# Attention scores in two passes of the rounded format, in a pool/attention/expert layer on one core

## The chip, the cores and the metric

The kernel runs on one core of one Trainium2 chip. The metric is the device time of one execution in microseconds (us). The kernel before takes 1535.73 us, the median of three runs (1535.3 to 1536.64).

## The reference, cut to what matters

One layer of a small diffusion transformer on 512 tokens of width 1024, with 256 context tokens. `x` and the context are normalised and modulated (scale and shift from `silu(c) @ ada_w`), multiplied by `w_in`, and split into a pooling half and q, k, v of eight attention heads of width 64. A query of a row sees 16 columns by 8 rows of neighbours, with a bias table, and all 256 context keys:

```python
s_loc = jnp.einsum('bwhd,biwjhd->bhwij', q_r, k_win).astype(jnp.float32) * scale + bias
s_ctx = jnp.einsum('bwhd,bchd->bhwc', q_r, k_ctx).astype(jnp.float32) * scale
s_all = jnp.concatenate([s_loc.reshape(B, H, GRID_W, n_loc), s_ctx], axis=-1)
prob = jax.nn.softmax(s_all, axis=-1)
```

The pooled half and the attention result go through `w_out` and back into `x`. After that comes a layer of 16384 experts, of which each token picks 16 per head by two sorted lists of keys; most of the kernel's time is there.

## The kernel before, in words

Numbers are float32. TensorE also takes a rounded float32 format, F32R. Large products are written as three matmuls in that format (`mm3`, L66 to L69): each operand is split into a rounded part (`hi`, a ScalarE copy) and the rest (`lo`, a VectorE subtraction), and hi·hi, hi·lo and lo·hi are summed in PSUM (`split`, L71; `load_split`, L82). The attention scores do not use this: they are plain float32 matmuls.

**Stages.** From the start to some 44 us the inputs are normalised and turned. From 44 to 174 us a loop over `g` in the order 4, 5, 6, 7, 0, 1, 2, 3 multiplies by eight column blocks of `w_in`: 4 and 5 give k, 6 and 7 give v, 0 and 1 the pooling half, 2 and 3 give q. The loop also builds the modulation rows chunk by chunk (`ada_more`, which chunk at which `g` is in `ADA_AT`). From 174 to about 256 us come 32 attention steps, one for each of four blocks of 128 queries and eight heads, with nine units of the `w_out` product (`out_unit`) mixed in by the table `units`. The rest of `w_out` and the second normalisation end near 306 us, and the expert layer fills the rest.

**k and q before.** `KT[j]` holds the keys of two heads in 128 partitions, for 512 tokens and 256 context keys, copied by ScalarE from PSUM (L437, L441). `QZ[j]` holds the queries of two heads in 128 partitions, each head in a copy of its own in which the other head's 64 rows were set to zero (L291, L292), scaled by -1/8 (`to_qz`). So one matmul over all 128 rows gives the scores of one head.

**One attention step before.** `scores` makes two float32 matmuls of 256 columns, local keys (L377, or L380 and L381 in the last block) and context keys (L383), into one PSUM bank ("S", two banks); one VectorE instruction adds the bias and finds the minimum of the negated scores (L389); ScalarE takes the exponential and its sum (L391). `turn`, two steps behind, transposes the 512 columns on TensorE (L463) into a bank of tag "T" (two banks) and ScalarE copies them out (L465). `values`, three steps behind, makes four float32 matmuls with v (L473). `BIA` holds nine bias tiles: one for each head and one of zeros for the context. The eight of the first three blocks are loaded at the start and the eight of the last block during the third; each is negated by ScalarE after its load (L369).

**What sets the order.** Outside the regions marked as scheduled by hand, a planner orders the instructions at build time, by the order of the program and by estimated times, and hands out buffers. Each engine then runs its list in that order. Loads of weights, biases and modulation chunks all stand in one list of DMA issues, SP's: an issue that waits for its buffer holds up those behind it. The expert layer is ordered by hand. Rings of buffers that the change touches: "raw" (3, loads of weights), "m8" (2: the context operands, later the pooled half and both parts of the third block of `w_out`), "cx" (2), "pool" (3, temporaries and the copies of L465), "xp" (4).

Of the kernel before, what the change touches and what calls it, by code (L numbers as in the profile page):

```python
# [6 lines left out]
F32 = mybir.dt.float32  # L7
# [3 lines left out]
I32 = mybir.dt.int32  # L11
# [41 lines left out]
def _build(tc, nc, es, A, out, taps):  # L53
# [28 lines left out]
    def load_split(src, t=None, pool=None):  # L82
        t = t or load_raw(src)
        hi = (pool or stream).tile([P, KC, 256], F32R, tag="m8" if pool else "whi", name="whi", bufs=2)
        lo = (pool or stream).tile([P, KC, 256], F32R, tag="m8" if pool else "wlo", name="wlo", bufs=2)
        split(t, hi, lo)
        return hi, lo
# [74 lines left out]
    QZ = [fp.tile([P, 2, SEQ], F32, name=f"qz{j}") for j in range(4)]  # L162
# [15 lines left out]
    def rstd_of(x, pool):  # L178
        st = pool.tile([P, 2], F32, tag="st", name="st", bufs=4)
        scr = pool.tile([P, D], BF, tag="pool", name="sq", bufs=3)  # L180
# [138 lines left out]
    ADA_AT = {6: 2, 7: 3, 1: 4, 3: 5}  # L319
# [10 lines left out]
    def pooling(g, x):  # L330
        w = WINDOWS[g]
        pw = fp.tile([P, P], F32, tag="pw", name="pw", bufs=2)
        nc.scalar.dma_start(pw, A["pool_w"][g])
        s = fp.tile([P, 528], F32, tag="pool", name="pl", bufs=3)
        nc.vector.tensor_add(s[:, 1:528], x[:, 0:527], x[:, 1:528])
        lo_, hi_ = 1, 528
        step = 1
        while step * 2 < w:
            s2 = fp.tile([P, 528], F32, tag="pool", name="pl", bufs=3)
# [6 lines left out]
        po = fp.tile([P, 512], F32, tag="pool", name="po", bufs=3)  # L346
# [26 lines left out]
    def scores(b, h):  # L373
        kt, qs = KT[h // 2], QZ[h // 2][:, h % 2, b * P:(b + 1) * P]
        sp = psf.tile([P, 512], F32, tag="S", name="ps")
        if b < 3:
            nc.tensor.matmul(sp[:, 0:256], qs, kt[:, b * P:b * P + 256], start=True, stop=True)  # L377
            kb = [b, b + 1, 4, 5]
        else:
            nc.tensor.matmul(sp[:, 0:128], qs, kt[:, 0:P], start=True, stop=True)  # L380
            nc.tensor.matmul(sp[:, 128:256], qs, kt[:, 384:512], start=True, stop=True)  # L381
# [5 lines left out]
        st = fp.tile([P, 1], F32, tag="ast", name="ast", bufs=6)  # L387
# [8 lines left out]
    def to_qz(jj, pt):  # L396
        for e in range(2):
            r = slice(e * 64, e * 64 + 64)
            act(QZ[jj][r, e, 0:384], pt[r, 64:448], AF.Copy, scale=-0.125)
            act(QZ[jj][r, e, 384:512].rearrange("p (a c) -> p a c", c=64), edges(pt[r, :]), AF.Copy, scale=-0.125)  # L400

    def early_scores():
        for n in range(H):
            ld_bias(n)
        for n in range(2):
            q1.append(scores(*steps[n]))

    for g in (4, 5, 6, 7, 0, 1, 2, 3):
# [15 lines left out]
        for k, j in order_kj(g):  # L424
            cs = slice(j * P, (j + 1) * P)
            if g == 3 and j == 1 and k == 0:
                to_qz(2, pzs[0])
                early_scores()
# [3 lines left out]
        for j in range(2):  # L432
# [3 lines left out]
            if sec == 2:  # L436
                act(KT[jj][:, :SEQ], pt, AF.Copy)  # L437
# [3 lines left out]
                act(KT[jj][:, SEQ:], pc[:, :CTX], AF.Copy)  # L441
            elif sec == 1:
                if jj != 2:
                    to_qz(jj, pt)
            else:
                xp = fp.tile([P, 528], F32, tag="xp", name="xp", bufs=4)
# [13 lines left out]
    def turn(b, h, pr, kb):  # L460
# [3 lines left out]
        pT = fp.tile([P, 528], F32, tag="pool", name="pT", bufs=3)[:, :512]  # L464
# [10 lines left out]
    def normalise(b):  # L475
        nc.vector.reciprocal(sums[b][:, 1, :], sums[b][:, 0, :])
        ob = fp.tile([P, 528], F32, tag="xp", name="ob", bufs=4)[:, :512]
# [16 lines left out]
    def out_unit(g, t):  # L494
# [6 lines left out]
        for k in range(KC):  # L501
            mm3(pt[:, :256], mixh[:, k, ts_], mixl[:, k, ts_],
                whi[:, k, :], wlo[:, k, :], k == 0, k == KC - 1)
# [66 lines left out]
    def scale2(t):  # L570
        st = fp.tile([P, 4], F32, tag="st2", name="st2", bufs=4)
        scr = fp.tile([P, D], BF, tag="pool", name="sq2", bufs=3)
# [141 lines left out]
    ED = persist.tile([P, P], I32, name="eD")  # L714
    GD = persist.tile([P, P], F32, name="gD")
# [185 lines left out]
    dots = persist.tile([P, P], F32, name="dots")  # L901
# [378 lines left out]
```

## Time and profile before

| what | value |
|---|---|
| median of three runs | 1535.73 us (1535.3 to 1536.64) |
| the profiled execution's own time | 1536.22 us |
| its span, first to last instruction | 1534.5 us |
| mean granted TensorE clock | 0.991 |
| busy: TensorE, weight loads, VectorE, ScalarE, GpSimd | 1502.8, 1347.2, 1203.8, 612.2, 343.3 us |

PE is TensorE's matmuls, PEld its weight loads (they run beside matmuls), DVE is VectorE, ACT ScalarE, SP the queue that issues DMAs. The recorded length of a matmul is more than what it costs in a row of matmuls, since they overlap: the price of one is read from start to start. A float32 matmul of the program shows as two records.

### The profile page before, as it was taken

The page shows a single profiled execution, that of the slowest core. Times are in us where ns is not written, and L with a number is a line of the kernel's source. Part 1 is how long each engine was busy: PE and PEld are TensorE (multiplying, and loading weights), DVE is VectorE, ACT ScalarE, POOL GpSimd, SP SyncE. Part 2 cuts the span into 40 slices and gives each one's busy share as a digit, 9 for nine tenths or more (in the row PEclk, how much of TensorE's full clock was granted, in tenths as well). Part 3 has the DMA queues.
Part 4 walks back from the last instruction along what each step waited for, and adds up shares of the span by engine and source line. Part 5 has one row for each costly group of instructions (what it writes and reads, how often), then busy time and mean ns, then how long its engine had stood idle before and what let it go on. Part 6 is the DMA issues. An engine that isn't in the chain of part 4 may idle for free.

```text
span 1534.5 us, 22100 instructions
## 1 busy us (share of the span) xinstructions
PE 1502.8 (98%) x8553; PEld 1347.2 (88%) x8553; DVE 1203.8 (78%) x2208; ACT 612.2 (40%) x893; POOL 343.3 (22%) x278
## 2 busy tenths in 40 slices
PE   7999999999999999999999999999999999999997
PEld 3897799888999999999898888898889889889886
DVE  7857533538999998976888888878888898888896
ACT  4423554423334455554333433423333333432343
POOL 0000000000000000000234435444445444444441
PEclk9999999999999999999999999999999999999999
DMA  9575300032235467877699999999999999998981
GB/s 378 183 279 208 114 25 5 28 120 94 99 125 189 178 230 291 319 299 275 219 359 383 348 354 351 379 314 354 345 362 336 372 359 373 331 349 321 375 300 56
DMA packets 136166, 398.25 MB, mean 260 GB/s; under 512 B 9334, under 2 KB 62198, under 8 KB 120828
## 3 DMA queue, kind: packets, MB, share of 16 engines
q1 hardware_dynamic: 92280, 225.10, 40.7%
q0 software_dynamic: 36864, 134.23, 23.7%
q10 hardware_dynamic: 6916, 37.49, 6.2%
q8 instruction: 67, 1.10, 0.3%
q14 instruction: 39, 0.32, 0.1%
HBM read 358.52 MB, written 38.28 MB: 259 GB/s over the span
## 4 chain that ended last, share of the span: by engine, by line
PE 53%; issue 8%; POOL 4%; DVE 3%; DMA 3%; ACT 1%; POOLq 0%; ACTq 0%; DVEq 0%
PE pa L69 9%; PE pa L67 9%; PE pa L68 9%; PE acc L67 8%; PE acc L68 8%; PE acc L69 8%; POOL gr L912 4%; DMA gr<-in_v,eD 3%; PE wp L853 3%; DVE wlo L553 1%; DVE gr L919 0%; ACT whi L547 0%; DVE gm L839 0%; DVE y L1073 0%; DVE y L1072 0%
## 5 line engine op out<-in xcount | busy, mean ns | idle before, releaser
L69 PE MATMUL pa<-h2hi,wlo 128*128 128x384 f32 (+1 forms) x1152 | 397.4, 345 | 3.8 <-DVE wlo L553 3.7
L67 PE MATMUL pa<-h2hi,whi 128*128 128x384 f32 (+1 forms) x1152 | 400.4, 348 | 0.0
L68 PE MATMUL pa<-h2lo,whi 128*128 128x384 f32 (+1 forms) x1152 | 396.7, 344 | 0.0
L67 PE MATMUL acc<-vh,wah 128*128 128x512 f32 x768 | 299.2, 390 | 1.4 <-ACT wah L1037 1.4
L68 PE MATMUL acc<-vl,wah 128*128 128x512 f32 x768 | 299.6, 390 | 0.0
L69 PE MATMUL acc<-vh,wal 128*128 128x512 f32 x768 | 298.8, 389 | 0.0
L912 POOL DMA_INDIRECT gr<-in_u,eD x128 | 158.7, 1240 | 520.4 <-ACT wah L1037 310.7
L69 PEld LDWEIGHTS pa<-h2hi,wlo 128*128 128x128 f32 x1152 | 217.6, 189 | 11.5 <-DVE wlo L553 5.5
L67 PEld LDWEIGHTS pa<-h2hi,whi 128*128 128x128 f32 x1152 | 217.8, 189 | 8.2
L68 PEld LDWEIGHTS pa<-h2lo,whi 128*128 128x128 f32 x1152 | 217.7, 189 | 8.0
L912 POOL DMA_INDIRECT gr<-in_v,eD x128 | 172.4, 1347 | 199.7 <-DVE accD L925 177.6
L925 DVE SCALAR_TENSOR_TENSOR accD<-gr,dots,accD 128x1024 f32<-128x1024 f32 x128 | 164.0, 1281 | 49.2 <-DMA gr<-in_v,eD 47.7
L919 DVE SCALAR_TENSOR_TENSOR gr<-gr,h2D 128x1024 f32<-128x1024 f32 x128 | 153.9, 1221 | 40.8 <-DMA gr<-in_u,eD 40.6
L553 DVE TENSOR_TENSOR wlo<-raw,whi 128x2048 fp32r<-128x2048 f32 x58 | 132.5, 2285 | 59.1 <-ACT whi L547 59.0
L69 PEld LDWEIGHTS acc<-vh,wal 128*128 128x128 f32 x768 | 144.2, 188 | 30.6 <-DVE wal L1044 0.3
L67 PEld LDWEIGHTS acc<-vh,wah 128*128 128x128 f32 x768 | 144.2, 188 | 29.8 <-ACT wah L1037 1.8
L68 PEld LDWEIGHTS acc<-vl,wah 128*128 128x128 f32 x768 | 144.1, 188 | 27.3
L1037 ACT ACTIVATE wah<-a 128x384 fp32r<-128x384 f32 x72 | 37.9, 526 | 203.4 <-DVE a L1035 203.3
L547 ACT ACTIVATE whi<-raw 128x2048 fp32r<-128x2048 f32 x58 | 110.8, 1910 | 14.4 <-ACT apair L685 6.3
L1019 ACT ACTIVATE vh<-raw 128x1024 fp32r<-128x1024 f32 x76 | 80.2, 1056 | 52.1 <-PE acc L69 52.0
L1026 DVE TENSOR_TENSOR vl<-raw,vh 128x1024 fp32r<-128x1024 f32 x76 | 92.5, 1217 | 1.2 <-ACT vh L1019 1.1
L1014 ACT ACTIVATE a<-pa 128x384 f32<-128x384 f32 x72 | 35.2, 489 | 118.6 <-PE pa L69 118.4
(260 smaller groups left out, 2071.3 us busy)
## 6 DMA issues: line engine op xcount, KB each, us to landing
raw<-in_u SPq DMA_DIRECT2D x50, 1024.0 KB, 5.0
raw<-in_v SPq DMA_DIRECT2D x38, 1024.0 KB, 9.5
vraw<-in_v SPq DMA_DIRECT2D x26, 1024.0 KB, 10.1
w_dram<-stg ACTq DMA_DIRECT2D x12, 2048.0 KB, 8.1
wt<-w_dram SPq DMA_DIRECT2D x32, 768.0 KB, 14.7
awr<-in_ada SPq DMA_DIRECT2D x16, 1024.0 KB, 4.8
vraw<-in_u SPq DMA_DIRECT2D x14, 1024.0 KB, 9.6
a_dram<-apair ACTq DMA_DIRECT2D x28, 384.0 KB, 3.7
```

The source lines that it names most:

```text
L67: nc.tensor.matmul(o, lh, rh, start=start, stop=False)
L68: nc.tensor.matmul(o, lh, rl, start=False, stop=False)
L69: nc.tensor.matmul(o, ll, rh, start=False, stop=stop)
L547: act(hi, raws[n], AF.Copy)
L553: nc.vector.tensor_sub(lo, raws.pop(n), parts[n][0].bitcast(F32))
L853: nc.tensor.matmul(wp[:, x, :], flat(ohj, 4 * q + x), flat(G[m], 4 * q + x), start=m == 0, stop=m == 1)
L912: nc.gpsimd.indirect_dma_start(out=r, out_offset=None, in_=A[kind], in_offset=bass.IndirectOffsetOnAxis(ap=ED[:, s:s + 1], axis=0))
L919: nc.vector.scalar_tensor_tensor(r, r, 1.0, h2D, op0=OP.mult, op1=OP.mult, accum_out=dots[:, s:s + 1])
L925: nc.vector.scalar_tensor_tensor(accD, r, wD[:, s:s + 1], accD, op0=OP.mult, op1=OP.add)
L1019: act(vh, vrs[seq[x]], AF.Copy)
L1026: nc.vector.tensor_sub(vl, vrs.pop(i), vs[i][0].bitcast(F32))
L1037: act(wah, avals[i], AF.Copy)
```

## The change

The rounded parts of the keys and the queries are made once, and the scores become two passes in F32R.

- `K2[h]`, one tile per head instead of one per two heads, holds the rounded key in the head's own 64 partitions and the rest of the key in the other 64. The rest is subtracted by VectorE into a temporary and moved across partitions by a DMA from SBUF to SBUF (`to_k2`). There are four `jj` and two parts (tokens, context), with two heads each: 16 copies, 16 subtractions and 16 DMAs in place of 8 copies.
- `QA[j]` holds the rounded query of each head twice, in both halves of the partitions (the second by a DMA); `QB` holds the rest of the query, in the head's own 64 partitions (`to_q`): 16 copies as before, 16 VectorE instructions and 8 DMAs more. The eight memsets of `QZ` go.
- A score is `QA · K2` over 128 rows, which sums rounded query times rounded key and rounded query times rest of key, plus `QB · K2` over the head's 64 rows. Four F32R matmuls of 256 columns take the place of two float32 matmuls of 256 columns; the last block's two pieces of 128 columns become one strided operand.
- The score has its own sign now: the maximum is found, and one small VectorE instruction negates it for the exponential. The bias needs no negation: its 16 ScalarE instructions go.
- `BIA` has three rotating tiles and the zeros. A bias is loaded for each of the 32 steps, three steps ahead.
- `xp` and `ob` move into the ring "pool", now of four buffers (seven in two rings before); `pw` has one buffer instead of two. `QB` takes one "m8" buffer, the third block of `w_out` has its rest in two "cx" buffers. Modulation chunk 5 is built at `g` 2 instead of 3. `ED`, `GD` and `dots` move to another pool.

```diff
     def load_split(src, t=None, pool=None):
...
+        if pool:
+            los = [pool.tile([P, KC // 2, 256], F32R, tag="cx", name="wlo2", bufs=2) for _ in range(2)]
+            act(hi, t, AF.Copy)
+            for n, lo in enumerate(los):
+                ks = slice(n * KC // 2, (n + 1) * KC // 2)
+                nc.vector.tensor_sub(lo, t[:, ks, :], hi[:, ks, :].bitcast(F32))
+            return hi, los
...
-    KT = [fp.tile([P, SEQ + CTX], F32, name=f"kT{j}") for j in range(4)]
-    for j in range(4):
-        nc.vector.memset(QZ[j][64:128, 0, :], 0.0)
-        nc.vector.memset(QZ[j][0:64, 1, :], 0.0)
+    K2 = [fp.tile([P, SEQ + CTX], F32R, name=f"k2_{h}") for h in range(H)]
+    QA = []
+    QB = []
+
+    def to_k2(jj, pt, dst, n):
+        lo = fp.tile([P, 512], F32R, tag="pr", name="klo", bufs=3)
+        for e in range(2):
+            h, r, o = 2 * jj + e, slice(e * 64, e * 64 + 64), slice(64 - e * 64, 128 - e * 64)
+            act(K2[h][r, dst], pt[r, :n], AF.Copy)
+            nc.vector.tensor_sub(lo[r, :n], pt[r, :n], K2[h][r, dst].bitcast(F32))
+            nc.sync.dma_start(K2[h][o, dst].bitcast(F32), lo[r, :n].bitcast(F32))
...
-    ADA_AT = {6: 2, 7: 3, 1: 4, 3: 5}
+    ADA_AT = {6: 2, 7: 3, 1: 4, 2: 5}
...
-    BIA = fp.tile([P, H + 1, 256], F32, name="bias")
-    nc.vector.memset(BIA[:, H, :], 0.0)
+    NB = 3
+    BIA = fp.tile([P, NB + 1, 256], F32, name="bias")
+    nc.vector.memset(BIA[:, NB, :], 0.0)
...
     def ld_bias(n):
         if n < len(steps):
             b, h = steps[n]
-            if b in (0, 3):
-                nc.sync.dma_start(BIA[:, h, :], A["bias"][h, b // 3])
-                act(BIA[:, h, :], BIA[:, h, :], AF.Copy, scale=-1.0)
+            nc.sync.dma_start(BIA[:, n % NB, :], A["bias"][h, b // 3])
...
     def scores(b, h):
-        kt, qs = KT[h // 2], QZ[h // 2][:, h % 2, b * P:(b + 1) * P]
+        k2, r = K2[h], slice(h % 2 * 64, h % 2 * 64 + 64)
+        qs = slice(b * P, (b + 1) * P)
+        qa, qb = QA[h // 2][:, h % 2, qs], QB[0][r, h // 2, qs]
...
-        nc.tensor.matmul(sp[:, 256:512], qs, kt[:, SEQ:SEQ + CTX], start=True, stop=True)
+        ol = sp[:, 0:256] if b < 3 else two(sp[:, 0:256])
+        for o, kk in ((ol, loc), (sp[:, 256:512], lambda z: z[:, SEQ:SEQ + CTX])):
+            nc.tensor.matmul(o, qa, kk(k2), start=True, stop=False)
+            nc.tensor.matmul(o, qb, kk(k2[r, :]), start=False, stop=True)
...
-        nc.vector.tensor_tensor_reduce(halves(pr), halves(sp), BIA[:, h::H - h, :], op0=OP.add, op1=OP.min,
-                                       scale=1.0, scalar=3.0e38, accum_out=st)
-        act(pr, pr, AF.Exp, bias=st, scale=-1.0, accum_out=sums[b][:, 0, h:h + 1])
+        i = steps.index((b, h)) % NB
+        nc.vector.tensor_tensor_reduce(halves(pr), halves(sp), BIA[:, i::NB - i, :], op0=OP.add, op1=OP.max,
+                                       scale=1.0, scalar=-3.0e38, accum_out=st[:, 0:1])
+        nc.vector.tensor_scalar(st[:, 1:2], st[:, 0:1], -1.0, None, op0=OP.mult)
+        act(pr, pr, AF.Exp, bias=st[:, 1:2], accum_out=sums[b][:, 0, h:h + 1])
...
-    def to_qz(jj, pt):
+    def to_q(jj, pt):
+        if not QB:
+            QA.extend(fp.tile([P, 2, SEQ], F32R, tag=f"qz{j}", name=f"qa{j}", bufs=1) for j in range(4))
+            QB.append(fp.tile([P, 4, SEQ], F32R, tag="m8", name="qb", bufs=2))
...
+                act(d(qa), z, AF.Copy, scale=0.125)
+                nc.vector.scalar_tensor_tensor(d(qb[r, :]), z, 0.125, d(qa.bitcast(F32)), op0=OP.mult, op1=OP.subtract)
+            nc.sync.dma_start(QA[jj][o, e, :].bitcast(F32), qa.bitcast(F32))
...
-            if n >= 2 * H:
-                ld_bias(n + H)
+            ld_bias(n + NB)
```

## Rows read from the trace of the kernel before

**Rows 1.** The page, parts 1 and 2: busy us of each engine; PE's busy tenths.
```profile
PE 1502.8 (98%) x8553; PEld 1347.2 (88%) x8553; DVE 1203.8 (78%) x2208; ACT 612.2 (40%) x893; POOL 343.3 (22%) x278
...
PE   7999999999999999999999999999999999999997
```
**Rows 2.** Stretches: us, busy us of PE, PEld, DVE, ACT, POOL, granted clock, DMA.
```profile
62.00:72.00 10.00, 10.00 (x56) 8.29 (x55) 8.83 (x16) 2.95 (x4) 0.00 (x0) 1.00 0.39 143
...
175.00:185.00 10.00, 8.83 (x61) 7.48 (x60) 9.21 (x12) 9.13 (x18) 0.00 (x0) 1.00 0.30 105
...
200.00:215.00 15.00, 15.00 (x116) 14.16 (x115) 5.23 (x15) 7.30 (x19) 0.00 (x0) 1.00 0.07 19
```
**Rows 3.** Timeline of PE over one attention step: start us, us, line, count.
```profile
199.26 0.65 PE L377 MATMUL ps<-kT,qz 128*128 128x256 f32 x2
199.75 0.59 PE L383 MATMUL ps<-kT,qz 128*128 128x256 f32 x2
200.18 0.60 PE L463 MATMUL tp<-small,pr 128*128 128x128 f32 x4
200.62 1.00 PE L473 MATMUL op<-vn,pT 128*128 128x64 f32 x8
201.46 0.65 PE L377 MATMUL ps<-kT,qz 128*128 128x256 f32 x2
```
**Rows 4.** Timeline of PE and PEld in a unit of the w_out product.
```profile
206.25 0.28 PE L67 MATMUL po<-whi,mixh 128*128 128x256 f32 x1
206.26 0.19 PEld L68 LDWEIGHTS po<-wlo,mixh 128*128 128x128 f32 x1
206.37 0.28 PE L68 MATMUL po<-wlo,mixh 128*128 128x256 f32 x1
...
208.59 0.28 PE L69 MATMUL po<-whi,mixl 128*128 128x256 f32 x1
```
**Rows 5.** Timeline of ACT where its work piles up as attention starts.
```profile
179.00 0.71 ACT L391 ACTIVATE pr<-pr,ast 128x512 f32<-128x512 f32 x1
...
181.50 0.72 ACT L391 ACTIVATE pr<-pr,ast 128x512 f32<-128x512 f32 x1
```
**Rows 6.** Timelines of PE, ACT and DVE as attention starts.
```profile
173.90 0.59 PE L377 MATMUL ps<-kT,qz 128*128 128x256 f32 x2
...
178.81 0.70 PE L377 MATMUL ps<-kT,qz 128*128 128x256 f32 x2 [0.94 <-DVE ast L389]
...
180.47 1.10 PE L473 MATMUL op<-vn,pT 128*128 128x64 f32 x8
...
161.75 1.93 ACT L72 ACTIVATE whi<-raw 128x2048 fp32r<-128x2048 f32 x1
...
177.18 1.91 ACT L456 ACTIVATE mixh<-psd 128x2048 fp32r<-128x2048 f32 x1
...
175.85 2.29 DVE L73 TENSOR_TENSOR wlo<-raw,whi 128x2048 fp32r<-128x2048 f32 x1 [0.20 <-ACT whi L72]
```
**Rows 7.** Groups by form, 0 to 420 us: busy us, mean ns, idle before.
```profile
L389 DVE CUSTOM_DVE_ANT_1 pr<-ps,bias 128x512 f32<-128x512 f32 x28 | 19.2, 690 | 26.8 <-PE ps L383 26.2 <-PE tp L463 0.6
...
L437 ACT ACTIVATE kT<-pz 128x512 f32<-128x512 f32 x4 | 2.4, 599 | 4.6 <-PE pz L69 4.5
...
L489 DVE TENSOR_TENSOR mixl<-pmix,mixh 128x512 fp32r<-128x512 f32 x4 | 2.8, 692 | 5.2 <-ACT mixh L488 5.2
...
L291 DVE MEMSET qz<- 64x512 f32 x4 | 1.9, 485 | 0.6 <-issue 0.2
```
**Rows 8.** Timeline of DVE in the key stage.
```profile
66.60 0.42 DVE L213 TENSOR_TENSOR clo<-vn,chi 128x256 fp32r<-128x256 f32 x1
...
79.28 0.75 DVE L128 TENSOR_SCALAR aacc<-awr,cc 128x1024 f32<-128x1024 f32 x1 [2.29 <-DMA awr<-in_ada]
```
**Rows 9.** The bias tile's 16 loads, from issue to landing.
```profile
DMA to landing us min/median/max: 2.0/2.2/3.2
```
**Rows 10.** Waits of SP's queue, 100 to 300 us: total, times, longest.
```profile
SPq L79 <- DVE wlo L73: 26.9, 4, 14.4
```

More of the change, by code (lines that the diff above doesn't have):

```diff
@@ L84, in load_split @@
         hi = (pool or stream).tile([P, KC, 256], F32R, tag="m8" if pool else "whi", name="whi", bufs=2)
-        lo = (pool or stream).tile([P, KC, 256], F32R, tag="m8" if pool else "wlo", name="wlo", bufs=2)
+        if pool:
[5 more added lines that the diff above has]
+            return hi, los
+        lo = stream.tile([P, KC, 256], F32R, tag="wlo", name="wlo", bufs=2)
         split(t, hi, lo)
@@ L161, in _build @@
     VN = [VNA[:, t, :] for t in range(6)]
-    QZ = [fp.tile([P, 2, SEQ], F32, name=f"qz{j}") for j in range(4)]
+    QZ = [fp.tile([P, 2, SEQ], F32, tag=f"qz{j}", name=f"qz{j}", bufs=1) for j in range(4)]
     hhi = persist.tile([P, KC, SEQ], F32R, tag="hhi", name="hhi")
@@ L338, in pooling @@
         while step * 2 < w:
-            s2 = fp.tile([P, 528], F32, tag="pool", name="pl", bufs=3)
+            s2 = fp.tile([P, 528], F32, tag="pool", name="pl", bufs=4)
             a, b = lo_ + step, hi_ - step
@@ L366, in ld_bias @@
             b, h = steps[n]
-            if b in (0, 3):
-                nc.sync.dma_start(BIA[:, h, :], A["bias"][h, b // 3])
-                act(BIA[:, h, :], BIA[:, h, :], AF.Copy, scale=-1.0)
+            nc.sync.dma_start(BIA[:, n % NB, :], A["bias"][h, b // 3])
     sums, ops = {}, {}
     def scores(b, h):
-        kt, qs = KT[h // 2], QZ[h // 2][:, h % 2, b * P:(b + 1) * P]
+        k2, r = K2[h], slice(h % 2 * 64, h % 2 * 64 + 64)
+        qs = slice(b * P, (b + 1) * P)
+        qa, qb = QA[h // 2][:, h % 2, qs], QB[0][r, h // 2, qs]
         sp = psf.tile([P, 512], F32, tag="S", name="ps")
+        two = lambda z: z.rearrange("p (a n) -> p a n", n=P)
         if b < 3:
-            nc.tensor.matmul(sp[:, 0:256], qs, kt[:, b * P:b * P + 256], start=True, stop=True)
+            loc = lambda z: z[:, b * P:b * P + 256]
             kb = [b, b + 1, 4, 5]
         else:
-            nc.tensor.matmul(sp[:, 0:128], qs, kt[:, 0:P], start=True, stop=True)
-            nc.tensor.matmul(sp[:, 128:256], qs, kt[:, 384:512], start=True, stop=True)
+            loc = lambda z: two(z[:, 0:512])[:, 0::3, :]
             kb = [0, 3, 4, 5]
-        nc.tensor.matmul(sp[:, 256:512], qs, kt[:, SEQ:SEQ + CTX], start=True, stop=True)
+        ol = sp[:, 0:256] if b < 3 else two(sp[:, 0:256])
+        for o, kk in ((ol, loc), (sp[:, 256:512], lambda z: z[:, SEQ:SEQ + CTX])):
+            nc.tensor.matmul(o, qa, kk(k2), start=True, stop=False)
+            nc.tensor.matmul(o, qb, kk(k2[r, :]), start=False, stop=True)
         if h == 0:
@@ L386, in scores @@
         pr = fp.tile([P, 512], F32, tag="pr", name="pr", bufs=3)
[L387 removed]
+        st = fp.tile([P, 2], F32, tag="ast", name="ast", bufs=6)
         halves = lambda z: z.rearrange("p (a n) -> p a n", n=256)
[L389 to L391 removed]
+        i = steps.index((b, h)) % NB
[3 more added lines that the diff above has]
+        act(pr, pr, AF.Exp, bias=st[:, 1:2], accum_out=sums[b][:, 0, h:h + 1])
         return b, h, pr, kb
     q1 = []
[L396 to L400 removed]
+    def to_q(jj, pt):
+        if not QB:
+            QA.extend(fp.tile([P, 2, SEQ], F32R, tag=f"qz{j}", name=f"qa{j}", bufs=1) for j in range(4))
+            QB.append(fp.tile([P, 4, SEQ], F32R, tag="m8", name="qb", bufs=2))
+        qb = QB[0][:, jj, :]
+        for e in range(2):
+            r, o = slice(e * 64, e * 64 + 64), slice(64 - e * 64, 128 - e * 64)
+            qa = QA[jj][r, e, :]
+            blk = lambda z: z.rearrange("p (a c) -> p a c", c=64)
+            for d, z in ((lambda t: t[:, 0:384], pt[r, 64:448]), (lambda t: blk(t[:, 384:512]), edges(pt[r, :]))):
+                act(d(qa), z, AF.Copy, scale=0.125)
+                nc.vector.scalar_tensor_tensor(d(qb[r, :]), z, 0.125, d(qa.bitcast(F32)), op0=OP.mult, op1=OP.subtract)
+            nc.sync.dma_start(QA[jj][o, e, :].bitcast(F32), qa.bitcast(F32))
     def early_scores():
[L403 removed]
+        for n in range(NB):
             ld_bias(n)
@@ L426, in _build @@
             if g == 3 and j == 1 and k == 0:
-                to_qz(2, pzs[0])
+                to_q(2, pzs[0])
                 early_scores()
@@ L436, in _build @@
             if sec == 2:
-                act(KT[jj][:, :SEQ], pt, AF.Copy)
+                to_k2(jj, pt, slice(0, SEQ), SEQ)
                 pc = psf.tile([P, 512], F32, tag="O", name="pz2")
@@ L440, in _build @@
                     mm3(pc[:, :CTX], whi[:, k, cs], wlo[:, k, cs], chi[:, k, :], clo[:, k, :], k == 0, k == KC - 1)
-                act(KT[jj][:, SEQ:], pc[:, :CTX], AF.Copy)
+                to_k2(jj, pc, slice(SEQ, SEQ + CTX), CTX)
             elif sec == 1:
                 if jj != 2:
-                    to_qz(jj, pt)
+                    to_q(jj, pt)
             else:
-                xp = fp.tile([P, 528], F32, tag="xp", name="xp", bufs=4)
+                xp = fp.tile([P, 528], F32, tag="pool", name="xp", bufs=4)
                 nc.vector.memset(xp[:, 0:8], 0.0)
@@ L713, in _build @@
                    allow_small_or_imprecise_dtypes=True)
-    ED = persist.tile([P, P], I32, name="eD")
-    GD = persist.tile([P, P], F32, name="gD")
+    ED = late.tile([P, P], I32, name="eD")
+    GD = late.tile([P, P], F32, name="gD")
     slots = {}
@@ L900, in _build @@
     accD = mp.tile([P, D], F32, name="accD")
-    dots = persist.tile([P, P], F32, name="dots")
+    dots = late.tile([P, P], F32, name="dots")
     wD = dots
```

16 lines of the change are left out of this document (8 added, 8 removed).

## The prediction

> **What bounds the kernel now.** I read the page first: TensorE is busy for 98% of the span, and in nine tenths or more of every slice but the first and the last [rows 1]. So whatever shortens TensorE's list shortens the kernel, if no other engine steps in. Then I asked for the stretches in which the change works. In the steady part of attention (200 to 215 us) TensorE is busy for all 15.00 us at a granted clock of 1.00, its 2.4 GHz level, while VectorE has 5.23 us of work and ScalarE 7.30. As attention starts (175 to 185) it is otherwise: VectorE 9.21 of 10 us, ScalarE 9.13, TensorE 8.83. In the key stage (62 to 72) TensorE is full and VectorE has 8.83 of 10 [rows 2]. The three stretches have different limits, so the change is priced in each by itself.
>
> The recorded length of a matmul says little, since matmuls overlap; I read from start to start. One step runs from 199.26 to 201.46, 2.20 us: 0.92 for the scores (two float32 matmuls of 0.43, and 0.06 at the start), 0.44 for four transposes, 0.84 for the values [rows 3].
>
> **The change part by part.** The sum is made against the profiled execution, 1536.22 us (span 1534.5 and 1.7 around it), which is 0.5 above the median of 1535.73.
>
> *The scores.* Two float32 matmuls go, four F32R matmuls of 256 columns come. Such matmuls stand in the `w_out` units: from 206.25 to 208.59 there are 20 of them from start to start, so 0.117 each, each with a weight load of its own [rows 4]. A step's scores then cost 4 x 0.117 + 0.06 = 0.53 instead of 0.92: 0.39 saved, 12.5 us in 32 steps, and a period of 1.81. Two of the four matmuls have only 64 rows, and no row shows that. Below, I bound them by one of the eight records of the values, 0.84 / 8 = 0.105 [rows 3], which would give 0.8 us more in all; above, by a float32 record of the same columns, 0.43 / 2 = 0.215, which takes 64 x 0.098 = 6.3 us back. I take 0.117, since columns, format and load are the same and only the rows differ. The last block's operand in one strided piece is taken at the same price.
>
> A rule speaks against this change here. The rows show a weight load of 0.19 us begun at 206.26, while the matmul begun at 206.25 is still on record, and the next matmul 0.12 after the last: a load of the whole array runs beside a matmul of the whole array [rows 4]. The Trainium skill (TensorE: Matmul & The Clock Gate, section "The mechanism") says that a weight load overlaps with matmuls in flight only when their row groups differ. By that rule the trace does not agree for full loads; for a 64-row load between full ones no row here shows it. What it would make of the time is a rival below.
>
> *Do ScalarE and VectorE keep up with 1.81?* When ScalarE has a pile of work, two steps of it (an exponential and a copy each) take from 179.00 to 181.50, 1.25 a step [rows 5]. VectorE has 0.69 for L389 [rows 7]; reading out the result and the new negation of one column are two small instructions, which I estimate at 0.3 together. The transposes come two steps behind the scores, 3.6 us, and the chain between (1.0 on VectorE, 0.9 on ScalarE, some 0.6 of hand-over) is 2.5. So the steady part stays TensorE's, and the saving is real there.
>
> *The start of attention.* Here part of it is lost. TensorE waits for VectorE at 178.81, behind a split of 2.29 us begun at 175.85, and begins the first values at 180.47, since ScalarE had 1.91 us of `mixh` at 177.18 [rows 6]. The four and a half steps of scores done between 173.90 and 180.47 are not what this waits for, so their 4.5 x 0.39 = 1.7 us come back as idle time. The bank of the last q block is held longer by a VectorE instruction on 64x384: 0.5 by columns from the 0.69 of L489, which bounds it above [rows 7]; below, 0. I take 0.5. The ScalarE split of the third `w_out` block stood at 161.75; now its buffer is free only after the instructions on the pooled half, `mixh` at 177.18 and the one after it [rows 6]. That is 1.9 us in the middle of ScalarE's pile: 0 if it falls beside a `w_out` unit, 1.9 without slack. I take 1.3.
>
> *The key stage.* ScalarE's copies grow from 8 to 16, of 0.60 and less [rows 7], some 4 us more on an engine with 2.95 in 10 [rows 2]: nothing. VectorE gets 16 subtractions, 8 of 0.69 (as L489) and 8 of 0.42 (as L213), 8.9 us, less eight memsets of 0.485, 3.9 [rows 7, 8]: 5.0 net. VectorE delivers the last context operand at 66.60 and later waits 2.29 us for a DMA [rows 8]; that and the memsets' place cover most of it. The first four subtractions fall before 66 us and hold both "S" banks some 2 to 3 us longer, while TensorE has context products to do. Bounds: 0, and 2.8 us if the four are paid in full. I take 0.7.
>
> *The queries* add 16 VectorE instructions, 8 of some 0.5 and 8 smaller, from 150 to 175 us; the next product in TensorE's list covers them, and without that cover they would cost some 6 us. I take nothing but the 0.5 above. The bias negations that go, the smaller ring for pooling, the moved modulation chunk and the single `pw` buffer change only what stands beside that product: nothing, and 1 us lost at most, if a pooling copy is late.
>
> *DMAs.* 24 moves within SBUF and 32 bias loads (16 before) stand in SP's list. A bias is issued after L389 of three steps before and lands in 2.2 us, at most 3.2 [rows 9]; three steps of 1.81 are 5.4, less 0.8 for L389: some 2 us to spare. For a move no row stands; I take the same 2.2, which only the last q block waits for, beside VectorE's and ScalarE's piles. 0.3 for both together; the upper end is the first rival.
>
> *Sum:* 12.5 - 1.7 - 0.5 - 1.3 - 0.7 - 0.3 = 8.0 us. What follows is TensorE's and starts earlier by that [rows 1]. So 1528.2 in a profiled execution, 1527.7 against the median.
>
> **The rivals.**
> - *SP's list blocks the biases.* Loads of the next weights stand in the same list and wait for their buffers: four of them waited 26.9 us in all, the longest 14.4 [rows 10]. Should the planner put such a load ahead of a bias that is needed soon, the scores stop until it is released. It decides from the 2 us of slack on; a wait of 14.4 in the wrong place costs 12.4, and the time is 1527.7 + 12.4 = 1540. For it: the list runs strictly in order, and the moves of the last q block stand in it too. Against: the planner orders by when it expects buffers to be free, and TensorE has few gaps by that order now.
> - *Weight loads go in series with matmuls once 64-row loads are among them.* A score matmul would then cost its 0.12 and the load's 0.19 [rows 4], 1.24 a step against 0.86 [rows 3]: 32 x 0.38 = 12.2 us slower, and with the other terms but the first two (2.8) about 1551. Against it speak the full loads of rows 4; nothing in the trace speaks for it. It is what the rule above would do here.
> - *The gain is half off the path*: hand-overs between VectorE and ScalarE hold a step at 2.0, half-way between 2.20 and 1.81. Then 27 steps give 0.2 each, 5.4, less 2.8 of other terms: 1533. For it: TensorE waits behind the two already at 178.81 [rows 6]. Against: 1.25 a step in a pile [rows 5].
> - *All is kept*: the planner reorders the start of attention and the key stage so that nothing comes back. 12.5: 1523.
>
> **How the numbers follow.** Forecast (1524 to 1532) 0.72; all kept 0.08; half off the path 0.10; SP's list 0.07; loads in series 0.03. About 0.2%, 3 us, is what a measurement of this kernel can tell from no change: faster is below 1532.7, slower above 1538.8. Faster: forecast, all kept and a third of "half off the path", 0.83. Same: the rest of that and some of SP's list, 0.09. Slower: 0.08. The range goes from 1522 (all kept, with the lower bound of the 64-row matmul) to 1535 (most of the 6.3 us of its upper bound, or half the gain and a late pooling copy).
>
> **What would show it.** In the steady part the transposes begin 0.5 us after the scores instead of 0.9, and steps are 1.81 apart; at 2.0 with TensorE idle before L463 or L473 the chain binds. The new score matmuls stand 0.117 apart; at 0.2 the 64-row pass is dear, at 0.3 the loads are in series. TensorE's idle time between the last q product and the steady part grows by some 3 us. A wait of L389 for the bias DMA shows SP's list. The key stage ends within 1 us of where it did. The prediction is wrong if the work after attention does not start some 8 us earlier, or if it does and the kernel gives it back later.

## The result and the profile after

| what | before (run beside it) | after |
|---|---|---|
| median | 1535.51 us (1533.75 to 1536.64) | 1576.51 us (1575.64 to 1579.86) |
| profiled execution, span | 1536.22, 1534.5 us | 1575.64, 1573.8 us |
| first to last score matmul | 166.2 to 254.5 us | 175.1 to 295.5 us |
| mean granted TensorE clock | 0.991 | 0.977 |

The change makes the kernel 2.7% slower: ratio 1.0271, interval 1.0254 to 1.0288. Forecast were 1527.7 us; 48.8 us lie between. The page, parts 1 and 2, answers to [rows 1]:

```profile
PE 1535.3 (98%) x8537; PEld 1363.3 (87%) x8537; DVE 1217.3 (77%) x2265; ACT 612.8 (39%) x885; POOL 346.0 (22%) x278
...
PEclk9999859999999999999999999999999999999999
```

TensorE is busy for 98% again: a full bar says nothing of what fills it. The tenths of the granted clock (`PEclk`) have an 8 and a 5 in the fifth and sixth slices, some 157 to 236 us. The stretches (columns as in [rows 2]) say where:

```profile
175.00:185.00 10.00, 10.00 (x40) 6.71 (x39) 4.28 (x14) 5.91 (x10) 0.00 (x0) 1.00 0.48 134
200.00:215.00 15.00, 15.00 (x53) 11.64 (x52) 2.59 (x10) 3.89 (x9) 0.00 (x0) 0.50 0.29 96
190.00:242.00 52.00, 50.79 (x191) 41.79 (x189) 14.64 (x45) 18.47 (x39) 0.00 (x0) 0.50 0.21 70
246.00:295.00 49.00, 49.00 (x342) 41.68 (x340) 18.20 (x59) 20.82 (x46) 0.00 (x0) 1.00 0.12 36
```

From 200 to 215 TensorE does 53 matmuls in the time of 116 before, at 0.50, its 1.2 GHz level. Even at full clock (246 to 295) its weight loads no longer fill the stretch. One step there in the timeline of PE answers to [rows 3]:

```profile
249.60 0.36 PE L402 MATMUL ps<-k,qa 128*128 128x256 f32 x1
249.90 0.38 PE L403 MATMUL ps<-k,qb 64*128 64x256 f32 x1
250.21 0.38 PE L402 MATMUL ps<-k,qa 128*128 128x256 f32 x1
250.52 0.39 PE L403 MATMUL ps<-k,qb 64*128 64x256 f32 x1
250.84 0.66 PE L493 MATMUL tp<-small,pr 128*128 128x128 f32 x4
251.33 1.00 PE L503 MATMUL op<-vn,pT 128*128 128x64 f32 x8
252.14 0.36 PE L402 MATMUL ps<-k,qa 128*128 128x256 f32 x1
252.44 0.38 PE L403 MATMUL ps<-k,qb 64*128 64x256 f32 x1
```

And in that of its weight loads:

```profile
252.43 0.18 PEld L403 LDWEIGHTS ps<-k,qb 64*128 64x128 f32 x1
```

The scores take 1.24 us (249.60 to 250.84) and the step 2.54 (to 252.14), against 0.92 and 2.20 before. All four matmuls are 0.31 apart, the 128-row ones too, and the load of 252.43 begins with its own matmul of 252.44, not beside the one before. At the lower clock a step takes 4.50 us:

```profile
208.81 0.56 PE L402 MATMUL ps<-k,qa 128*128 128x256 f32 x1
...
213.31 0.56 PE L402 MATMUL ps<-k,qa 128*128 128x256 f32 x1
```

The waits of TensorE from 50 to 300 us (total, times, longest; the others add 1.9):

```profile
PE pz L67 <- DVE klo L307: 3.2, 1, 3.2
PE tp L493 <- DVE qb L429: 1.2, 1, 1.2
```

The stretches at the longest of them and behind it, then VectorE's list there, with the split ahead of the subtraction (`klo`) that TensorE waits for:

```profile
72.00:76.00 4.00, 1.23 (x7) 1.26 (x8) 3.66 (x5) 1.59 (x4) 0.00 (x0) 0.91 0.80 288
76.00:80.00 4.00, 4.00 (x13) 3.10 (x13) 3.27 (x4) 0.59 (x1) 0.00 (x0) 0.66 0.65 184
```

```profile
71.87 2.29 DVE L73 TENSOR_TENSOR wlo<-raw,whi 128x2048 fp32r<-128x2048 f32 x1 [0.49 <-ACT whi L72]
74.19 1.38 DVE L307 TENSOR_TENSOR klo<-pz,k 64x256 fp32r<-64x256 f32 x3
```

So the 49 us between forecast and result hold only some 6 us of waiting. After the attention all of it is shifted: the expert layer's first product starts at 577.5 instead of 537.4 us.

### The profile page after: what moved, and what is told of

It reads as the page before. It is cut to its first block, busy times and chain, and to the rows that moved or that the text cites. A ratio compares the mean times of both kernels' runs of the same rounds, so it can differ in the third digit from the quotient of the medians.

```text
span 1573.8 us, 22210 instructions
## 1 busy us (share of the span) xinstructions
PE 1535.3 (98%) x8537; PEld 1363.3 (87%) x8537; DVE 1217.3 (77%) x2265; ACT 612.8 (39%) x885; POOL 346.0 (22%) x278
## 3 DMA queue, kind: packets, MB, share of 16 engines
q1 hardware_dynamic: 96504, 229.82, 40.7%
## 4 chain that ended last, share of the span: by engine, by line
PE 53%; issue 8%; POOL 4%; DVE 3%; DMA 1%; ACT 0%; POOLq 0%; ACTq 0%; DVEq 0%
PE pa L69 9%; PE pa L67 9%; PE pa L68 9%; PE acc L67 8%; PE acc L68 8%; PE acc L69 8%; POOL gr L941 4%; PE wp L882 3%; DMA gr<-in_u,eD 1%; DVE wlo L582 1%; DVE gm L868 0%; DVE y L1102 0%; ACT whi L576 0%; DVE prd L804 0%; DVE pos L682 0%
```

## Experiments

Each ran beside the kernel before; ratios are to that, with 95% intervals. Theory A: the 64-row loads put loads and matmuls in series. B: the granted clock is what costs most. C: the key stage costs more than 0.7 us.

### Full rows in the second pass

```diff
-        qa, qb = QA[h // 2][:, h % 2, qs], QB[0][r, h // 2, qs]
+        qa, qb = QA[h // 2][:, h % 2, qs], QB[0][:, h // 2, qs]
-            nc.tensor.matmul(o, qb, kk(k2[r, :]), start=False, stop=True)
+            nc.tensor.matmul(o, qb, kk(k2), start=False, stop=True)
```

The score now also takes in the rest of the other head's query times the rest of this head's key. Every engine's list keeps its order.

> The second pass of a score runs over all 128 rows (the other 64 rows multiply the neighbour head's rest of query by this head's rest of key, a term of the size of float32 rounding). Nothing else changes, the order of every engine's list included. Theory A, the loads of 64 rows keep weight loads from running beside matmuls: score matmuls stand 0.12 us apart instead of 0.31, a step in the steady part takes 1.8 us instead of 2.54, 32 x 0.73 = 23 us less. If the low clock of 188 to 242 us is a consequence of that (theory B), it goes too and gives some 24 us more: about 1530. If the clock falls anyway (rival of B, the idle time and the order of the list do it): about 1550. Rival of A, the new operands or their strides are slow, not the row count: 0.31 stays, 1576.

Measured: 1537.11 us (1534.41 to 1539.66), ratio 1.0014 [1.0001, 1.0027]. One step of PE:

```profile
200.91 0.36 PE L402 MATMUL ps<-k,qa 128*128 128x256 f32 x1
201.11 0.28 PE L403 MATMUL ps<-k,qb 128*128 128x256 f32 x1
201.23 0.28 PE L402 MATMUL ps<-k,qa 128*128 128x256 f32 x1
201.35 0.28 PE L403 MATMUL ps<-k,qb 128*128 128x256 f32 x1
201.47 0.60 PE L493 MATMUL tp<-small,pr 128*128 128x128 f32 x4
...
202.72 0.36 PE L402 MATMUL ps<-k,qa 128*128 128x256 f32 x1
```

The load that belongs to the second of these:

```profile
201.00 0.19 PEld L403 LDWEIGHTS ps<-k,qb 128*128 128x128 f32 x1
```

Twice the rows in half of the matmuls, and 39.4 us less. The spacing is 0.12, the load of 201.00 runs ahead of its matmul of 201.11, and the step is 1.81, as forecast. A is shown. The clock is low here too, but only for 7 us, between 184 and 192.

### Half rows in the kernel before

```diff
-        kt, qs = KT[h // 2], QZ[h // 2][:, h % 2, b * P:(b + 1) * P]
+        r = slice(h % 2 * 64, h % 2 * 64 + 64)
+        kt, qs = KT[h // 2][r, :], QZ[h // 2][r, h % 2, b * P:(b + 1) * P]
```

> The kernel before, its float32 scores unchanged but for the rows: each head's matmuls take only the 64 rows that hold something (the other half of the q tile is zero). Theory (a 64-row load among 128-row loads isn't hidden): a score set has 4 loads of 0.19 us, all hidden before; in series they add 0.76 us to a step, 24 us over 32 steps: 1559, and up to 1585 if the clock falls as it did in the changed kernel. Rival (the series belongs to the rounded format, or to the two passes of unequal height alone): no difference, 1535 (1532 to 1539).

Measured: 1545.73 us (1543.43 to 1546.94), ratio 1.0059 [1.0036, 1.0082]. One step of PE, then a stretch of 50 us:

```profile
214.40 0.70 PE L378 MATMUL ps<-kT,qz 64*128 64x256 f32 x2
214.94 0.59 PE L384 MATMUL ps<-kT,qz 64*128 64x256 f32 x2
215.46 0.66 PE L464 MATMUL tp<-small,pr 128*128 128x128 f32 x4
215.95 1.00 PE L474 MATMUL op<-vn,pT 128*128 128x64 f32 x8
216.88 0.70 PE L378 MATMUL ps<-kT,qz 64*128 64x256 f32 x2
```

```profile
200.00:250.00 50.00, 50.00 (x356) 42.99 (x355) 16.71 (x44) 23.14 (x55) 0.00 (x0) 1.00 0.08 22
```

Fewer rows make this kernel slower as well, so it is not a matter of the format. But the step grows by 0.28 us (2.48 against 2.20), not by the 0.76 of four loads in series, and 32 x 0.28 = 9.0 us. The clock stays at 1.00: 64-row loads alone don't bring it down. In a step of this order the row count changes only twice, into the set and out of it. The time lies between theory and rival; neither was right in size.

### Both passes of a kind together

```diff
-        for o, kk in (...):
-            nc.tensor.matmul(o, qa, kk(k2), start=True, stop=False)
-            nc.tensor.matmul(o, qb, kk(k2[r, :]), start=False, stop=True)
+        for o, kk in parts_:
+            nc.tensor.matmul(o, qa, kk(k2), start=o is ol, stop=False)
+        for o, kk in parts_:
+            nc.tensor.matmul(o, qb, kk(k2[r, :]), start=False, stop=o is not ol)
```

> Only the order of a score set changes: both q_hi passes first, then both 64-row q_lo passes, so two changes of the row count per set instead of four. If every load next to a 64-row load runs in series (0.31 us a matmul, as in the changed kernel), the set stays near 1.24 us and the time is that of the changed kernel, 1576 (1570 to 1581). If only a change of the row count costs, two of the four matmuls go back to 0.12: 0.38 us a step at full clock, some 12 us over 32 steps, more if the low clock of 188 to 242 us goes with it: 1545 to 1565.

Measured: 1558.82 us (1555.11 to 1560.49), ratio 1.0143 [1.0117, 1.0170]. One step of PE, then two stretches:

```profile
253.96 0.40 PE L403 MATMUL ps<-k,qa 128*128 128x256 f32 x2
254.29 0.50 PE L405 MATMUL ps<-k,qb 64*128 64x256 f32 x2
254.72 0.66 PE L495 MATMUL tp<-small,pr 128*128 128x128 f32 x4
255.22 1.00 PE L505 MATMUL op<-vn,pT 128*128 128x64 f32 x8
256.03 0.48 PE L403 MATMUL ps<-k,qa 128*128 128x256 f32 x2
```

```profile
190.00:225.00 35.00, 33.79 (x142) 30.16 (x142) 11.15 (x34) 13.41 (x28) 0.00 (x0) 0.50 0.23 74
227.00:285.00 58.00, 58.00 (x461) 53.41 (x459) 22.37 (x73) 26.42 (x59) 0.00 (x0) 1.00 0.13 35
```

The same four matmuls in another order take 0.76 instead of 1.24 us (253.96 to 254.72) and the step 2.07. So a change between 128 and 64 rows has a price, and two fewer are worth 0.48 us at full clock; the two that are left cost 0.26 (2.07 against 1.81 with full rows), so it isn't one price for each. 32 x 0.48 is 15.4 us; what makes it the measured 17.7 is a balance that no run takes apart: the clock was low for 37 us instead of 54, and waits for the turn's copy and for `ob` add some 2.5 us. A load of 64 rows behind one of 64 rows is hidden again; the second of the set begins 0.11 ahead of its matmul:

```profile
254.40 0.19 PEld L405 LDWEIGHTS ps<-k,qb 64*128 64x128 f32 x1
254.51 0.28 PE L405 MATMUL ps<-k,qb 64*128 64x256 f32 x1
```

### Dense work against the low clock

`dense` adds 24 F32R matmuls of full rows at the sixth step, which the planner places at the start of the attention; `dense_9` the same before the tenth step, bound there by its weights. The results are not used.

```diff
+            if n == 9:
+                act(dzw, q2[-1][2][:, 0:128], AF.Copy)
+                dz = ps1.tile([P, 512], F32, tag="p1", name="dz")
+                for k in range(24):
+                    nc.tensor.matmul(dz[:, :256], dzw, K2[1][:, 0:256], start=k == 0, stop=k == 23)
```

> 24 F32R matmuls of 256 columns over full rows, whose result nothing uses, are added among the score matmuls just before the place where the clock fell; the 64-row passes stay. They cost 2.8 us. Theory B in its narrow form, the weak run of twelve score matmuls in series made the clock fall there: with dense work in that place it stays at 1.00 and some 24 us come back, about 1555. Rival, steps with 64-row passes cannot hold the clock without a unit of dense matmuls among them: it falls a few us later and stays low until the first unit of the w_out product, about 1577.

> The changed kernel (64-row passes) with 24 more full-row matmuls of 256 columns in one piece before the tenth step, bound to that place by their weights, a copy of that step's turned probabilities; their result is not used. They cost 24 x 0.12 to 0.24 us, 2.8 to 5.6 us. If dense full-row work is what brings the clock back, the granted clock rises to 1.00 at about 210 us instead of 242, some 7 steps go from 4.5 to 2.5 us (14 us), and the time falls to 1566 (1562 to 1571). Rival (the clock comes back by time, not by work): it stays at 0.50 to about 242 us and the time is 1580 (1577 to 1583).

Measured: `dense` 1573.80 us (1573.67 to 1578.27), ratio 1.0263 [1.0235, 1.0292]; `dense_9` 1567.39 us (1561.41 to 1569.05), ratio 1.0203 [1.0188, 1.0217]. Stretches of `dense`, then of `dense_9`:

```profile
188.00:196.00 8.00, 6.79 (x55) 6.24 (x54) 5.37 (x13) 5.48 (x11) 0.00 (x0) 1.00 0.57 182
198.00:235.00 37.00, 37.00 (x132) 29.32 (x131) 8.79 (x31) 11.04 (x26) 0.00 (x0) 0.50 0.18 57
```

```profile
189.00:192.00 3.00, 3.00 (x16) 3.00 (x16) 2.97 (x4) 1.55 (x4) 0.00 (x0) 0.50 0.49 136
192.00:193.00 1.00, 1.00 (x10) 1.00 (x9) 0.97 (x2) 0.70 (x2) 0.00 (x0) 0.80 1.03 434
...
209.00:270.00 61.00, 61.00 (x418) 51.40 (x418) 22.93 (x73) 26.56 (x59) 0.00 (x0) 1.00 0.14 40
```

In `dense` the rival came: the clock held through the piece, fell after the next wait (1.21 us for a difference of the query, until 195.79), and stayed down until 242, in a `w_out` unit. In `dense_9` it was back at 192 to 193, in transposes and values, before the added piece ran at 205; so that run does not test what lifts the clock. It is of use all the same: its profiled execution, the fastest of four, shows the attention with hardly any low clock, 176.8 to 277.9 us; the other three, at a mean clock of 0.982 to 0.983 against its 0.992, took 5 to 8 us more. Less 24 x 0.12 = 2.8 for the piece that is 98.3 us, against 120.4 after the change and 79.7 with full rows. So of the 40.7 us between the last two, about 22 are clock and 19 are loads in series. By the steps, some 50 us more of low clock x 1.96 / 4.50 make 22 too; the 19 are less than 32 x 0.73 = 23, since the run with full rows has 2.4 us more of waits in the attention and 3.5 us more of low clock. B is right for half of it. That the low clock follows from A is not shown: with full rows it shrinks to 7 us, but `dense_9` keeps the loads in series and has 4, and `before_64` has 64-row loads and none.

### The key stage

Four versions relieve the bank or VectorE there: `k_freed` and `full_k` copy the key product to SBUF first (64-row and full passes); `full_ord` lets ScalarE copy both heads before VectorE subtracts; `full_pool` copies first and lets GpSimd subtract (both do the same for the queries); `full_ada` is `full_ord` with two modulation chunks one block later. All but `k_freed` have full rows. The code is cut to the key stage.

```diff
+        raw_ = fp.tile([P, 528], F32, tag="pool", name="kraw", bufs=4)   # k_freed, full_k
+        act(raw_[:, :n], pt[:, :n], AF.Copy)
...
+        for h, r, o in he:                                               # full_ord
+            act(K2[h][r, dst], pt[r, :n], AF.Copy)
+        for h, r, o in he:
+            nc.vector.tensor_sub(lo[r, :n], pt[r, :n], K2[h][r, dst].bitcast(F32))
...
+            nc.gpsimd.tensor_sub(lo[r, :n], raw_[r, :n], K2[h][r, dst].bitcast(F32))   # full_pool
...
-    ADA_AT = {6: 2, 7: 3, 1: 4, 2: 5}                                    # full_ada
+    ADA_AT = {7: 2, 0: 3, 1: 4, 2: 5}
```

> In the key stage ScalarE first copies each product from PSUM to SBUF, and the rounded part and the rest are made from that copy, so the PSUM bank is free after one instruction. Theory C, the late bank of the key product (TensorE waited 3.2 us for the subtraction, and its clock fell after that) is what delays the stage: the copy of the last value product moves from 125.9 to some 120 us, and the time falls by 5 to 7 us, if the clock of attention stays as it is. Rival, VectorE's list or SP's list is what is late: nothing changes, or the three extra ScalarE copies of each block make it worse by 1 or 2 us.

> Both edits, full rows in the second pass and the key product copied out first. If A, B and C hold: about 1530 less 5 to 7, 1523 to 1525, 10 to 12 us below the kernel before, near the forecast of the prediction. If the key stage's delay has another cause: 1530.

> Full rows in all score passes, and for each key and query product ScalarE makes both heads' rounded copies first and VectorE both differences after, instead of in turns (no operation more or less). If the turns on one bank (ScalarE waiting for VectorE 0.3 to 4.8 us at a time) cost the late first score of the full-row kernel (175.2 against 166.2 us), the first score moves to 168 to 172 and the time to 1530 (1526 to 1534). Rival (VectorE simply has too much to do ahead of it: modulation chunk, split, differences): the turns hide behind that, 1537 (1534 to 1540) as with full rows alone.

> Full rows, and the key and query products are copied out of their bank by ScalarE at once; the differences are made by GpSimd, which is idle in that stretch, from the copy: some 16 x 0.55 us of the key stage and 16 x 0.42 us of the query stage leave VectorE, 5 us or more come to ScalarE. If VectorE's list is what makes the start of the attention late, the first score moves to 167 to 171 us and the time to 1529 (1524 to 1533). Rival (ScalarE, or GpSimd's slower differences, are late instead, or the buffers of the copies are waited for): 1537 (1534 to 1545).

> Full rows, both heads' copies first, and two of the four modulation chunks one block of the input projection later (chunk 2 with block 7, chunk 3 with block 0), so that VectorE has about 10 us less to do in the key stage. If VectorE's load there makes the start of the attention late, the waits for klo and prow between 70 and 100 us go and the first score moves from 173 to 168 us; the time is 1531 (1527 to 1535). Rival (the load is only moved and is late at the pooling instead): 1537 (1534 to 1541).

> The kernel before with the same later modulation chunks (2 with block 7, 3 with block 0, 5 with block 2), nothing else. The trace of before shows no wait of TensorE in the key stage, so there is nothing to win: no difference, 1535.5 (1533 to 1538). Rival (the gain of the full-row version with later chunks has nothing to do with the score passes): 1530 (1527 to 1533).

`before_ada` is the kernel before with the chunk table of `full_ada`.

| kernel | median us (range) | ratio [interval] | first v copy | first score |
|---|---|---|---|---|
| k_freed | 1573.55 (1570.03 to 1577.49) | 1.0254 [1.0221, 1.0287] | 85.9 | 170.5 |
| full_k | 1534.03 (1530.93 to 1539.82) | 1.0000 [0.9985, 1.0015] | 86.3 | 172.9 |
| full_ord | 1536.88 (1532.65 to 1542.01) | 1.0008 [0.9993, 1.0022] | 87.6 | 171.3 |
| full_pool | 1538.34 (1535.30 to 1541.75) | 1.0016 [1.0003, 1.0030] | 92.7 | 176.6 |
| full_ada | 1530.95 (1527.95 to 1532.75) | 0.9958 [0.9946, 0.9971] | 84.1 | 165.8 |
| before_ada | 1533.85 (1530.83 to 1541.19) | 0.9987 [0.9973, 1.0001] | 83.4 | 164.4 |

The last two columns (us in the profiled execution) are read from the copies of v and the score matmuls; for the kernels before, after and with full rows (the scores alone) these rows are (first and last start stand after the durations)

```profile
L421 ACT ACTIVATE vn<-pz x12: 384/385/387, 85.1 to 117.8; 128x256 f32<-128x256 f32 x12
```

```profile
L451 ACT ACTIVATE vn<-pz x12: 383/384/387, 91.2 to 125.9; 128x256 f32<-128x256 f32 x12
L402 PE MATMUL ps<-k,qa x64: 275/384/582, 175.1 to 295.2; 128*128 128x256 f32 x64
```

```profile
L402 PE MATMUL ps<-k,qa x64: 276/284/387, 175.2 to 254.8; 128*128 128x256 f32 x64
```

The changed key stage makes the v product 6 us late and the first score 9. Freeing the bank gets 5 us back at the v product, but part is given away again: in `full_k` TensorE then waits 2.2 us for the modulation row (`prow`), whose sum on VectorE is late. The time of `k_freed` is 3.0 us below that after the change, not 5 to 7 as expected, and the intervals of the two ratios overlap; its clock is low for 58 us. Letting the two engines take turns less often (`full_ord`) gets 3.9 of the 9 us back by the first score, and the later chunks (`full_ada`) the other 5.5: the waits for `klo`, `clo` and `prow` are gone, and the first score stands at 165.8, 0.4 ahead of the kernel before. That execution of the kernel before had its clock at 0.50 from 139 to 142 us; `before_ada`, which had not, has its first score at 164.4, so against this control 1.4 us of the delay are left. So both the shared bank and VectorE's list are in it; how much of the 5.5 is the list, and how much the chunk table by itself, these single executions don't settle. C is shown. What `full_ord` wins by the first score it loses in the attention, 83.3 us (171.3 to 254.6) against 79.7, with a low clock of 13.5 us instead of 7. `full_pool` was a miss: the v product came at 92.7, with a wait of 2.3 us for a v copy on ScalarE, which had the added copies. The control `before_ada` is inconclusive: at most 0.3% for the chunk table by itself.

### The start of the attention

`full_late` is `full_ord` with the split of the pooled half of the mix behind the seventh step; `full_both` has the later chunks too; `full_gp` is `full_ada` with this split and that of the first block of `w_out` on GpSimd.

```diff
-    act(mixh[:, 0:4, :], pooled[0], AF.Copy)
-    nc.vector.tensor_sub(mixl[:, 0:4, :], pooled[0], mixh[:, 0:4, :].bitcast(F32))
...
+        if n == 6:                                                       # full_late, full_both
+            act(mixh[:, 0:4, :], pooled[0], AF.Copy)
+            nc.vector.tensor_sub(mixl[:, 0:4, :], pooled[0], mixh[:, 0:4, :].bitcast(F32))
...
+    nc.gpsimd.tensor_copy(mixh[:, 0:4, :], pooled[0])                    # full_gp
+    nc.gpsimd.tensor_sub(mixl[:, 0:4, :], pooled[0], mixh[:, 0:4, :].bitcast(F32))
```

> Full rows, both heads' copies first, and the split of the pooled half of the mix (1.9 us on ScalarE, 2.3 us on VectorE) stands behind the seventh step instead of ahead of the first. If this split and the query differences in front of the first exponentials are what stops TensorE 3.4 us at 180 us and lets its clock fall, that wait goes below 1 us, the low clock of 183 to 197 us goes, and the time is 1529 (1526 to 1533). Rival (the turn's copy is late for another reason: the split of the output weights and four query copies stand ahead of it all the same): the wait stays over 2 us, 1537 (1534 to 1540).

> Both of these edits. If each theory holds, the gains add: first score at 168, no low clock at the start of the attention, 1524 (1520 to 1529), below the kernel before. If neither does, 1537 (1533 to 1541).

> The full-row version with the modulation chunks later, and the splits of the pooled half of the mix and of the first block of the output weights made by GpSimd, idle in that stretch, instead of ScalarE and VectorE (3.8 and 4.6 us of them stand ahead of the first turned probabilities). If these splits are what is left of the late start of the attention, TensorE's wait for the turn's copy goes from 3.4 to below 1 us, its clock holds 1.00 where it was 0.50 from 178 to 190 us (some 6 us), and the time goes from 1531 to 1524 (1521 to 1528). Rival (the eight query copies and differences alone stop it, or GpSimd's splits come too late for the first output unit): the wait stays or a new one stands at the output unit, 1531 (1528 to 1536).

Measured: `full_late` 1533.48 us (1527.67 to 1536.02), ratio 0.9966 [0.9952, 0.9981]; `full_both` 1531.27 (1527.16 to 1533.14), 0.9968 [0.9956, 0.9980]; `full_gp` 1533.75 (1528.30 to 1536.49), 0.9973 [0.9959, 0.9987]. The wait for the turn's copy, in `full_ada` and then in `full_both`:

```profile
PE tp L496 <- ACT pT L498: 3.4, 1, 3.4
```

```profile
PE tp L494 <- ACT pT L496: 1.6, 1, 1.6
```

The split is part of the wait (3.4 to 1.6), not all of it, and the gains don't add: `full_both` isn't faster than `full_ada`. The granted clock falls to 0.50 in every one of these versions there, for 7 (`full_both`), 14 (`full_ada`) and 17 us (`full_late`, `full_gp`). In `full_gp` the wait is 0.9, and a new one took its place, 2.9 us for the query's difference. VectorE and GpSimd:

```profile
175.41 5.91 DVE L73 TENSOR_TENSOR wlo<-raw,whi 128x2048 fp32r<-128x2048 f32 x1
...
174.65 4.53 POOL L494 TENSOR_TENSOR mixl<-psd,mixh 128x2048 fp32r<-128x2048 f32 x1
```

VectorE's split took 5.91 us beside GpSimd's, against 2.29 [rows 6], and ended 2.1 after it; the query's differences queued behind it.

## Why the prediction was wrong

- **The step that failed** is the price of the score matmuls: "I take 0.117, since columns, format and load are the same and only the rows differ", bounded above at 0.215. They stand 0.31 apart, the 128-row ones too, so a step's scores cost 1.24 us where I had 0.53: 32 x 0.71 = 22.7 us at full clock. The bound was of the wrong kind. It came from records of other matmuls, while the cost is in what a load may run beside; an upper bound for that was the rival's 0.12 + 0.19, which is what came.
- **The rival with 0.03** named mechanism and price (1.24 a step) rightly. I set "against it speak the full loads of rows 4", but a row of 128-row loads among 128-row loads says nothing of a mixed sequence, as I had noted myself. A rule of the Trainium skill (TensorE: Matmul & The Clock Gate, "The mechanism") is that a load overlaps with matmuls in flight only when the row groups differ. The runs don't agree for loads of the same rows: full ones among full ones are hidden, and 64-row ones behind 64-row ones. Read as "when they share no row group", as the rival took it, they agree for the mixed ones: 64 rows among 128 share a part, and stand 0.31 apart. Full rows in place of half rows (39.4 us), and the grouped order (17.7), show that the change between the two is what costs.
- **The rival's time, 1551, was 25 us short**, since it has no term for the clock, and the key stage at 0.7 too. After the change the clock went to 0.50 at 188 us, behind six score sets in series, the last three in a row, and a wait of 0.34, and came back at 242, in the first `w_out` unit; a step at 0.50 takes 4.50 us (208.81 to 213.31) against 2.54. About 22 us of the attention are this. The stretches of [rows 2] have a granted clock of 1.00, and I did not ask what the sum would be if that fell, though the trace of before has it at 0.50 elsewhere, from 44 to 49 and 139 to 142 us.
- **The attention without the two** came out right: with full rows it takes 79.7 us, and the forecast's terms for it (12.5 - 1.7 - 0.5 - 1.3 - 0.3) make 88.3 - 8.7 = 79.6. The steady step is 1.81, as forecast. That the total fits to 0.1 is luck in part: it holds 7 us of low clock, which the forecast has not, and waits of 3.9 us where the kernel before has 0.9. So the parts at the start erred against each other.
- **The key stage** was taken at 0.7, bounds 0 to 2.8; with what it makes late it costs 9 by the first score. The VectorE instructions were sized rightly (0.69 and 0.42), and put beside an idle time of 2.29 us [rows 8]. But they stand among the modulation chunk, the operands' split and the last context operands: the subtraction that TensorE needs waited behind a split of 2.29 us (3.2 us of TensorE, and a clock of 0.66 after it), and the chunk in turn came late. I added up VectorE's load over the stage instead of following its list. The version with copies first and the chunks elsewhere gives the 9 us back, or all but 1.4 against its own control.
- **Nothing** from the bias list: the loads land in 2.0 to 2.1 us and L410 never waited for one after the change. That rival falls.

The sum: 8.2 us up to the first score (8.9 where 0.7 was forecast) and 40.8 of attention (120.4 against 79.6) make 49.0 at the last score. Behind the attention the profiled execution gets 1.6 back and ends 47.4 above its forecast of 1528.2; by the medians it is the 48.8. Not settled is what lets the clock fall and what keeps it low for 54 us in one program and for 4 in another with the same steps (`dense_9`, and by the mean clocks not in every execution of it), and so how much of the spread of the full-row versions is due to it. In `k_freed` it fell at 181 us with no wait in the 9 us before, behind score sets in series:

```profile
172.00:181.00 9.00, 9.00 (x37) 6.06 (x35) 4.43 (x16) 6.07 (x9) 0.00 (x0) 1.00 0.32 81
181.00:238.00 57.00, 55.79 (x209) 45.92 (x210) 18.98 (x48) 21.70 (x48) 0.00 (x0) 0.50 0.23 72
```

The best version, `full_ada`, is 0.42% [0.29, 0.54] faster than the kernel before; about a third of that may be the chunk table alone.

## What to carry to other kernels

Before narrowing a matmul to the rows that hold something, look at what stands beside it in TensorE's list: a change of row count between neighbours can cost more than the rows save, and a harmless product in the spare rows cost nothing here (0.12 a matmul). Price such a step from a row that has the same neighbours, and where none exists, let the worst mechanism, not the nearest record, set the range. Follow the list of an engine near its limit, instruction by instruction, from the one that TensorE waits for; spare time elsewhere in the stage doesn't cover it. And any new series or wait in a stage at full clock may be charged twice, once for itself and once at 1.2 GHz, as here (19 and 22 us).

## What the runs showed of the hardware

- F32R matmuls of 256 columns with 128 and 64 rows in turns stood 0.31 us from start to start, and the load began with its own matmul; among 128-row ones it was 0.12, with the load 0.11 ahead; a 64-row load behind a 64-row one was 0.11 ahead too.
- Two two-input operations on tiles of 128x2048, one on VectorE and one on GpSimd at once, took 5.91 and 4.53 us; VectorE's alone takes 2.29. The Trainium skill (GPSIMD Engine Reference, "Key points") says that GpSimd shares its SBUF interfaces with VectorE and that they contend where VectorE has two SBUF inputs; this trace agrees.
- In every version with two passes the granted clock fell to 0.50 at the start of the attention, for 4 to 58 us, in most behind waits of 0.34 us (after the change) to 3.4, in `k_freed` behind none; the kernel before has a wait of 0.94 there [rows 6] and kept 1.00.
